# A decoder layer with a mixture of experts on one core: the residual rebuilt on VectorE in the first unit, rooms for the embedding kept a few at a time, the router's bias later

## The chip, the cores and the metric

The kernel runs on one core of a Trainium2 chip, as one program. The time is device microseconds of one execution; lower is better. Besides the timed executions one execution was run under the profiler, and every row below comes from that one.

## What is computed

One layer over 512 tokens of width 1024, all in float32. The part that matters here is the second half:

```python
x = layer_norm(alpha * x + merged @ w_o[i], ln1_g[i], ln1_b[i])
moe_out = hierarchical_moe(x, w_rg[i], b_rg[i], w_re[i], b_re[i], w_eg[i], w_eu[i], w_ed[i])
ple = jax.nn.sigmoid(x @ w_pg[i]) * (p[i] @ w_pp[i])
x = layer_norm(alpha * x + moe_out + ple, ln2_g[i], ln2_b[i])
```

Each token goes to one of 4 groups and there to 2 of 8 experts. An expert is a gated MLP, `(silu(x @ w_eg) * (x @ w_eu)) @ w_ed`, with 6 MB of weights; all 32 experts are read, about 201 MB. The term `ple` is called the embedding below: two matrix products, with w_pg (4 MB) and w_pp (1 MB), and the input p.

## The kernel before

Up to about 290 us of the profile stand the input projections, the attention and the pooling mixer; there TensorE is busy nearly all the time. Then follow three stretches.

**The output projection, the first norm and the router** (to about 380 us). The four blocks of 128 tokens are multiplied with w_o in two halves of 512 columns. The first half is scheduled by the framework, the second is in an order written by hand. The router's weights are multiplied by the norm's gain; the norm's offset becomes a bias of the router's logits, which eight narrow matmuls (`rb_ps`, L468, with the column `bcol` of the offset and the router's weights `wrr`) work out. `x1` is the normed x, kept as a high and a low half whose columns are stored in another order (`turned`); `acc` is the float32 residual to which the experts' results are added.

**The first unit** (about 377 to 417 us). A unit is a group of experts that are worked on together. KINDS = "ppppqqqpppppp": a p has 2 experts and up to 64 tokens each, a q has 4 experts and up to 32 tokens each; units are counted from 0, so units 4, 5 and 6 are the q. In a unit, `inner` multiplies the gathered tokens with w_eg (n = 0) and w_eu (n = 1), `h` is the gated product (ScalarE and VectorE, L1036 and L1037), TensorE turns it (`hT_ps`, L1050), `outer` multiplies with w_ed (L1099), `weighted` applies the gates' weights, and the scatter (L1132) adds the result to `acc`, one unit later. `gather` (L830) collects the tokens of the next two units in every second unit. In the first unit `relabel` (L731 to L741, VectorE) turns the router's tables into the experts' order; it works in the pool `lnt`, and the pool `ex`, in which `h` lives, takes the same memory, so that the first instruction on `h` waits for relabel's end. `renew` (L882) makes `acc` anew from the two halves of x1, four additions of 128x1024 on GpSimd, and ScalarE multiplies them by alpha.

**The stream of weights.** The 192 chunks of 1 MB of the experts' weights are loaded by SyncE's queue (L539), strictly in order, each into a room of 8 KB per partition; before a load is issued, the chunk that held the room must have been used by its last matmul. In the steady state there are 14 rooms: 8 of the kind s8 and 6 others. `eload_past` hands the rooms of used chunks on to the next loads.

**The embedding** borrows s8 rooms. `kept` counts those that were not handed on, up to the limit `keep`:

```python
            if tag == "s8" and kept[0] < keep[0]:
                kept[0] += 1
            elif tag != "acc":
                free.append(tag)
```

The limit is set to 8 at the start of unit 3. The generator `embedding` is advanced by `embed(i)` at six places of a unit, 0 to 5: after the first halves of the two `inner` (0 and 2), after the first product on h (1), ahead of `outer` (3), in its middle (4) and at the end (5). The table EMB gives how many steps each place takes. Steps 1 to 6 load p, add x1's halves into float32 rows (`xf`, GpSimd) and turn both; then come four quarters, each a split of the weights (`pgh` on ScalarE, `pgl` on GpSimd, L1179 and L1180; the next quarter's load is issued behind it) and four matrix steps of 30 matmuls (`pg_ps`). After unit 6 all rooms are handed back.

Of the kernel before, what the change touches and what calls it, by code (L numbers as in the profile page):

```python
# [31 lines left out]
ALPHA = 2.0 ** 0.25  # L32
# [4 lines left out]
def layer_kernel(ctx: ExitStack, tc: tile.TileContext, x, p, w_in, w_pool, pool_scale, w_pu, w_au,  # L37
                 w_o, ln1_g, ln1_b, w_rg, b_rg, w_re, b_re, w_eg, w_eu, w_ed, w_pg, w_pp,
                 ln2_g, ln2_b, out):
    nc = tc.nc  # L40
# [314 lines left out]
    with tc.manual_schedule():  # L355
# [12 lines left out]
        for k, eng in zip(range(4), (nc.vector, nc.gpsimd, nc.vector, nc.gpsimd)):  # L368
            hi, lo = (t[:, k] for t in first)
# [36 lines left out]
    for half in range(2):  # L406
        for br, (w, ah, al) in enumerate(((wpu, poh, pol), (wau, aoh, aol))):
            hi, lo = wnext()
            for c in range(4):
# [4 lines left out]
                o = mm()  # L414
# [17 lines left out]
    x1, acc = {}, {}  # L432
# [10 lines left out]
    lnt = lnt_cm.__enter__()  # L443
# [19 lines left out]
    nc.sync.dma_start(gcol, ln1_g[0].rearrange("(k p) -> p k", p=128))  # L463
    nc.sync.dma_start(bcol, ln1_b[0].rearrange("(k p) -> p k", p=128))

    o = tt("rb_ps")
    for k in range(KD):
        nc.tensor.matmul(o[:, :36], bcol[:, k:k + 1].to_broadcast([128, 128]), wrr[:, k], start=k == 0,  # L468
                         stop=k == KD - 1)

    lbias = lnt.tile([128, 40], F32, name="lbias")
    nc.vector.memset(lbias, -3.0e38)
    nc.vector.tensor_add(lbias[:, :4], rbias[:, :4], o[:, :4])
    nc.vector.tensor_add(lbias[:, 8:], rbias[:, 4:], o[:, 4:36])
    nc.vector.tensor_mul(wrr, wrr, gcol[:, :, None].to_broadcast([128, KD, 36]))
    wr2 = lnt.tile([128, KD, 72], F32R, name="wr2")
    nc.scalar.activation(wr2[:, :, :36], wrr, AF.Copy)
    nc.vector.tensor_sub(wr2[:, :, 36:], wrr, wr2[:, :, :36].bitcast(F32))
    fold = lnt.tile([128, 40], F32, name="fold")
    nc.vector.memset(fold, 0.0)  # L480
    nc.vector.tensor_add(fold[:, :4], ident[:, :4], ident[:, 36:40])
    nc.vector.tensor_add(fold[:, 8:], ident[:, 4:36], ident[:, 40:72])
# [269 lines left out]
    def residual(tb, half, o):  # L752
        cs = slice(half * 512, (half + 1) * 512)
        nc.vector.scalar_tensor_tensor(acc[tb][:, cs], acc[tb][:, cs], ALPHA, o[tb], op0=OP.mult, op1=OP.add)
        nc.vector.bn_stats(stats[:, tb, half], acc[tb][:, cs])
# [44 lines left out]
            out_proj(tb, 0, o, parts, range(4 * kk, 4 * kk + 4))  # L800
    for tb in range(NT):
        residual(tb, 0, o)
    o = [mm() for _ in range(NT)]
    parts = [wnext() for _ in range(2)]
    eload_first(8)
# [71 lines left out]
    def renew(b):  # L877

        new_acc(b)
        for tb in (b, b + 1):  # L880
            hi, lo = (x1[tb][:, i].rearrange("p (k m) -> p m k", k=KD).bitcast(F32) for i in range(2))
            nc.gpsimd.tensor_add(acc[tb].rearrange("p (m k) -> p m k", k=KD), hi, lo)  # L882

    def inner(j, n, o, ks):

# [10 lines left out]
    with tc.manual_schedule():  # L896
# [107 lines left out]
    def pair(j, other, extra):  # L1004
# [5 lines left out]
        def embed(i):  # L1010
            for _ in range(extra[i]):
                next(emb)

        h = ex.tile([128, FE], F32, name="h", bufs=1)

# [34 lines left out]
            nc.tensor.transpose(hp[:, f * 128:(f + 1) * 128], h[:, f * 128:(f + 1) * 128], ident)  # L1050
        hT = ex.tile([128, 4, 128], F32, name="hT", tag="h", bufs=1)
        nc.scalar.activation(hT, hp.rearrange("p (f s) -> p f s", f=4), AF.Copy)
        if j == 0:
            renew(2)
            for tb in range(NT):
                nc.scalar.activation(acc[tb], acc[tb], AF.Copy, scale=ALPHA)
        if last:
            split_acc(1)
        elif not four:
# [76 lines left out]
    def embedding():  # L1136
# [5 lines left out]
                nc.sync.dma_start(r, w[:, :, cs])  # L1142
            return raw

        def rows(tb):
            xf = s8([128, D], F32, "xf")
            nc.gpsimd.tensor_add(xf, x1[tb][:, 0].bitcast(F32), x1[tb][:, 1].bitcast(F32))
            return xf

        assert kept[0] >= 3  # L1150
        pr = s8([128, NT, 256], F32, "pr")
        nc.sync.dma_start(pr, p[0, 0].rearrange("(b t) c -> t b c", t=128))
        xf = [rows(tb) for tb in range(2)]
# [82 lines left out]

    EMB = {3: (0, 0, 0, 0, 0, 1), 4: (1, 1, 1, 1, 1, 2), 5: (1, 2, 1, 2, 1, 2), 6: (1, 2, 1, 2, 1, 2)}
    with tc.manual_schedule():  # L1240
# [123 lines left out]
```

## Time and profile before

| what | value |
|---|---|
| median of 3 runs (lowest, highest) | 905.2 us (904.72, 906.07) |
| the profiled execution, and its span | 910.67 us, 908.9 us |
| TensorE busy | 834.2 us (92%) |
| VectorE, ScalarE, GpSimd busy | 424.9, 216.0, 206.5 us |
| read from HBM | 239 MB, 265 GB/s over the span |
| granted TensorE clock, mean | 0.957 of full |

The profiled execution took 5.5 us longer than the median of the runs; the span is what the rows cover. TensorE is busy by far the longest, but busy says little where it runs at the lower clock (1.0 in the rows is 2.4 GHz, 0.5 is 1.2 GHz) or waits in short pieces between the chunks of the weights.

### The profile page before, as it was taken

Reading aid. Unit: us, or ns where it says so; the run is one execution under the profiler, and the core shown is the slowest. Engines: PE = TensorE matmul, PEld = TensorE weight load, DVE = VectorE, ACT = ScalarE, POOL = GpSimd, SP = SyncE. Lnnn points to the kernel's source line nnn. Section 1 sums busy time; section 2 is a strip of 40 time slices with the busy share of each in tenths; the row PEclk is TensorE's granted clock in tenths of the full one; section 3 lists DMA queues with packets and bytes.
Section 4 is the critical chain, followed back from the end, with each engine's and each line's share of the span. In section 5 each row is a group of like instructions: output and inputs, shape, how many; then the busy total and the mean of one; then the engine's idle time right before and its main releaser. Section 6 shows DMA issues by size and latency. Waiting matters only on the chain.

```text
span 908.9 us, 11416 instructions
## 1 busy us (share of the span) xinstructions
PE 834.2 (92%) x4382; PEld 528.0 (58%) x4382; DVE 424.9 (47%) x701; ACT 216.0 (24%) x447; POOL 206.5 (23%) x180
## 2 busy tenths in 40 slices
PE   8999898999999997849999988989879999999993
PEld 6886676677778786613644523657547454553642
DVE  4278557454468559581544332121121334423447
ACT  3124345444451125111110212101210110010124
POOL 3333233232312327260002202120321000000045
PEclk9999999999999898779999989999998999999997
DMA  7431312122215876457998699999997999999962
GB/s 243 138 93 48 88 52 82 58 60 80 90 50 197 263 288 241 173 234 304 420 410 346 235 414 416 408 408 419 377 420 313 419 419 419 418 420 420 420 245 95
DMA packets 65786, 241.87 MB, mean 266 GB/s; under 512 B 12096, under 2 KB 32576, under 8 KB 41408
## 3 DMA queue, kind: packets, MB, share of 16 engines
q1 hardware_dynamic: 65728, 241.10, 68.4%
q8 instruction: 36, 0.59, 0.3%
q14 instruction: 22, 0.18, 0.1%
HBM read 238.99 MB, written 2.10 MB: 265 GB/s over the span
## 4 chain that ended last, share of the span: by engine, by line
PE 44%; DMA 7%; issue 3%; POOL 1%; DVE 1%; ACT 1%; SPq 0%; POOLq 0%; ACTq 0%; DVEq 0%
PE mm L891 17%; PE mm L1099 10%; PE sc_ps L1132 5%; PE xg_ps L830 5%; DMA ew<-in_w_eu_dram 2%; DMA ew<-in_w_ed_dram 2%; PE pg_ps L142 2%; PE pg_ps L143 2%; PE pg_ps L144 2%; DMA ew<-in_w_eg_dram 2%; POOL pgl L1180 1%; DMA pr<-in_p_dram 1%; PE hT_ps L1050 1%; PE gt_ps L870 1%; ACT pgh L1179 0%
## 5 line engine op out<-in xcount | busy, mean ns | idle before, releaser
L891 PE MATMUL mm<-ew,xg 128*64 128x512 f32 (+1 forms) x1024 | 195.4, 604 | 9.1 <-DMA ew<-in_w_eu_dram 7.7
L891 PEld LDWEIGHTS mm<-ew,xg 128*64 128x64 f32 (+1 forms) x1024 | 58.0, 128 | 132.0 <-issue 112.3
L1099 PE MATMUL mm<-ew,hT 128*64 128x512 f32 (+1 forms) x512 | 100.0, 605 | 2.9 <-DMA ew<-in_w_ed_dram 2.0
L131 POOL TENSOR_TENSOR wlo<-wraw,whi 128x1024 fp32r<-128x1024 f32 x23 | 68.5, 2978 | 108.7 <-DVE whi L126 52.1
L142 PE MATMUL mm<-xth,whi 128*128 128x512 f32 x224 | 91.6, 409 | 0.0
L144 PE MATMUL mm<-xth,wlo 128*128 128x512 f32 x224 | 88.6, 396 | 0.0
L143 PE MATMUL mm<-xtl,whi 128*128 128x512 f32 x224 | 88.3, 394 | 0.0
L1037 DVE TENSOR_TENSOR h<-mm,h 128x512 f32<-128x512 f32 x26 | 18.0, 692 | 132.4 <-PE mm L891 69.4
L830 PEld LDWEIGHTS xg_ps<-G,x 128*128 128x128 f32 x448 | 57.6, 202 | 11.4 <-issue 7.4
L1133 DVE TENSOR_TENSOR acc<-acc,sc_ps 128x512 f32<-128x512 f32 x96 | 59.6, 681 | 5.6 <-PE sc_ps L1132 5.0
L1099 PEld LDWEIGHTS mm<-ew,hT 128*64 128x64 f32 (+1 forms) x512 | 27.8, 128 | 59.0 <-issue 52.1
L830 PE MATMUL xg_ps<-G,x 128*128 128x256 f32 (+1 forms) x448 | 60.9, 296 | 0.0
L1121 POOL TENSOR_TENSOR accl<-acc,acch 128x512 fp32r<-128x512 f32 x8 | 10.9, 1384 | 164.8 <-ACT acch L1120 164.8
L142 PEld LDWEIGHTS mm<-xth,whi 128*128 128x128 f32 x224 | 42.7, 191 | 9.5 <-issue 0.9
L144 PEld LDWEIGHTS mm<-xth,wlo 128*128 128x128 f32 x224 | 42.7, 190 | 9.4
L143 PEld LDWEIGHTS mm<-xtl,whi 128*128 128x128 f32 x224 | 43.0, 192 | 8.8 <-issue 0.5
L1200 DVE TENSOR_TENSOR sg<-pg_ps,sg 128x256 f32<-128x256 f32 x16 | 6.8, 425 | 83.3 <-ACT sg L1199 83.3
L143 PE MATMUL pg_ps<-pgl,xT 128*128 128x256 f32 x128 | 38.1, 298 | 7.3 <-POOL pgl L1180 7.3
L126 DVE CAST whi<-wraw 128x2048 fp32r<-128x2048 f32 x22 | 26.9, 1225 | 34.1 <-PE mm L143 16.6
L1132 PE MATMUL sc_ps<-yh,Gt 128*128 128x512 f32 x96 | 40.6, 423 | 1.6 <-DVE sg L1200 1.6
L142 PE MATMUL pg_ps<-pgh,xT 128*128 128x256 f32 x128 | 38.8, 303 | 2.5 <-ACT pgh L1179 2.5
L131 DVE TENSOR_TENSOR wlo<-wraw,whi 128x1024 fp32r<-128x1024 f32 x23 | 38.8, 1686 | 1.0
(270 smaller groups left out, 1372.3 us busy)
## 6 DMA issues: line engine op xcount, KB each, us to landing
ew<-in_w_eg_dram SPq DMA_DIRECT2D x64, 1024.0 KB, 11.6
ew<-in_w_eu_dram SPq DMA_DIRECT2D x64, 1024.0 KB, 12.3
ew<-in_w_ed_dram SPq DMA_DIRECT2D x62, 1024.0 KB, 13.5
wraw<-in_w_in_dram SPq DMA_DIRECT2D x15, 1024.0 KB, 5.5
wraw<-in_w_o_dram SPq DMA_DIRECT2D x4, 1024.0 KB, 5.1
pgr<-in_w_pg_dram SPq DMA_DIRECT2D x4, 1024.0 KB, 14.5
wraw<-in_w_pu_dram SPq DMA_DIRECT2D x2, 1024.0 KB, 5.1
wraw<-in_w_au_dram SPq DMA_DIRECT2D x2, 1024.0 KB, 5.0
```

Source lines behind the costliest of these rows:

```text
L126: nc.vector.tensor_copy(hi, wraw[i])
L131: eng.tensor_sub(lo[:, j], wraw[i][:, j], hi[:, j].bitcast(F32))
L142: nc.tensor.matmul(o, lh, rh, start=start, stop=False)
L143: nc.tensor.matmul(o, lh, rl, start=False, stop=False)
L144: nc.tensor.matmul(o, ll, rh, start=False, stop=stop)
L830: nc.tensor.matmul(o[:, kx * 256:kx * 256 + n], x1[tb][:, i, cs], G[tb // 2][:, tb % 2].rearrange("p u s -> p (u s)"), start=whole and tb ...
L891: nc.tensor.matmul(o[i * c:(i + 1) * c], xgs[j][:, k, i * c:(i + 1) * c], ew[chunk0[j] + ne * (2 * n + k // 4) + i][:, k % 4], start=k == ...
L1037: nc.vector.tensor_mul(ht, o, ht)
L1099: nc.tensor.matmul(o[i * n:(i + 1) * n], hT[:, f, i * n:(i + 1) * n], ew[chunk0[j] + ne * (4 + f // 2) + i][:, f % 2, halves[c]], start=f ...
L1121: nc.gpsimd.tensor_sub(l, acc[tb][:, halves[c]], h.bitcast(F32))
L1132: nc.tensor.matmul(o, Gt[:, tb * 128:(tb + 1) * 128], y[c][i], start=i == 0, stop=i == 1)
L1133: nc.vector.tensor_add(acc[tb][:, cs], acc[tb][:, cs], o)
```

## The change

Three things. The router's bias and folded weights are written behind the first half of the output projection instead of ahead of it. `renew` adds on VectorE, and both its calls and the multiplication by alpha stand together in unit 0, behind the tables `Gw` and ahead of `outer`. The embedding keeps its rooms by a table KEEP, in steps from the end of unit 2 on; `xf` takes one room for two blocks; the table EMB deals the 26 steps out in another way.

```diff
-    o = tt("rb_ps")
-    for k in range(KD):
-        nc.tensor.matmul(o[:, :36], bcol[:, k:k + 1].to_broadcast([128, 128]), wrr[:, k], start=k == 0,
-                         stop=k == KD - 1)
...
     for tb in range(NT):
         residual(tb, 0, o)
+
+    ob = tt("rb_ps")
+    for k in range(KD):
+        nc.tensor.matmul(ob[:, :36], bcol[:, k:k + 1].to_broadcast([128, 128]), wrr[:, k], start=k == 0,
+                         stop=k == KD - 1)
...
-            nc.gpsimd.tensor_add(acc[tb].rearrange("p (m k) -> p m k", k=KD), hi, lo)
+            nc.vector.tensor_add(acc[tb].rearrange("p (m k) -> p m k", k=KD), hi, lo)
...
         relabel(rk, weigh())
-        renew(0)
...
             for _ in range(extra[i]):
                 next(emb)
+            keep[0] = KEEP.get((j, i), keep[0])
...
-        if j == 0:
-            renew(2)
-            for tb in range(NT):
-                nc.scalar.activation(acc[tb], acc[tb], AF.Copy, scale=ALPHA)
...
         if not last:
             Gw = weights_of(j)
+        if j == 0:
+            for b in (0, 2):
+                renew(b)
+                for tb in (b, b + 1):
+                    nc.scalar.activation(acc[tb], acc[tb], AF.Copy, scale=ALPHA)
...
-        def rows(tb):
-            xf = s8([128, D], F32, "xf")
-            nc.gpsimd.tensor_add(xf, x1[tb][:, 0].bitcast(F32), x1[tb][:, 1].bitcast(F32))
-            return xf
+        def rows(b):
+            xf = s8([128, 2, D], F32, "xf")
+            for i in range(2):
+                nc.gpsimd.tensor_add(xf[:, i], x1[b + i][:, 0].bitcast(F32), x1[b + i][:, 1].bitcast(F32))
+            return [xf[:, i] for i in range(2)]
...
-    EMB = {3: (0, 0, 0, 0, 0, 1), 4: (1, 1, 1, 1, 1, 2), 5: (1, 2, 1, 2, 1, 2), 6: (1, 2, 1, 2, 1, 2)}
+    EMB = {3: (0, 0, 0, 1, 0, 0), 4: (1, 1, 1, 1, 1, 1), 5: (2, 2, 1, 2, 2, 1), 6: (2, 2, 1, 2, 1, 1)}
+
+    KEEP = {(2, 5): 2, (3, 3): 4, (3, 5): 5, (4, 0): 6, (4, 1): 7, (4, 2): 8}
...
-            if j in (min(EMB), NU - 2):
+            if j == NU - 2:
                 keep[0] = 8
```

What this does to the order is shown at three places. The first is VectorE in unit 0, behind the products on `h`; `Gt` is the turned table of the gates, which the scatter needs. Before:

```order
L741 TENSOR_TENSOR ranked<-by_slot 128x128
L1037 TENSOR_TENSOR h<-mm,h 128x512 x2
L862 TENSOR_TENSOR Gw<-iota_c,posm 128x512
L864 TENSOR_TENSOR Gw<-Gw,comb 128x512
L873 TENSOR_SCALAR Gt<-gt_ps 128x512
```

And now:

```order
L1037 TENSOR_TENSOR h<-mm,h 128x512 x2
L862 TENSOR_TENSOR Gw<-iota_c,posm 128x512
L864 TENSOR_TENSOR Gw<-Gw,comb 128x512
L882 TENSOR_TENSOR acc<-x_2688 128x1024
L882 TENSOR_TENSOR acc<-x_2742 128x1024
L882 TENSOR_TENSOR acc<-x_2925 128x1024
L882 TENSOR_TENSOR acc<-x_2928 128x1024
L873 TENSOR_SCALAR Gt<-gt_ps 128x512
```

The four additions left GpSimd, where they stood directly ahead of the first `xf`, and stand on VectorE ahead of `Gt`.

The second is SyncE's queue at the turn from unit 3 to unit 4. ew_3618 is chunk 55, the next two are chunks 56 and 57, the first of unit 4's w_eu; in brackets is whose counters a row waits for (DMAHW are earlier DMAs). Before:

```order
L539 DMA ew_3618<-in_w_eg_dram 128x2048 [waits DMAHW6_49,PE_49]
L539 ISA
L539 DMA ew_3744<-in_w_eu_dram 128x2048 [waits DMAHW7_49,PE_49]
L539 ISA
L539 DMA ew_3746<-in_w_eu_dram 128x2048 [waits DMAHW0_49,PE_49]
L1152 DMA pr_3786<-in_p_dram 128x4x256 [waits DMAHW1_49]
L539 ISA
L539 DMA ew_3818<-in_w_eu_dram 128x2048 [waits DMAHW2_49,PE_49]
```

And now:

```order
L521 DMA ew_3618<-in_w_eg_dram 128x2048 [waits DMAHW6_49,PE_49]
L521 ISA
L521 DMA ew_3628<-in_w_eu_dram 128x2048 [waits DMAHW7_49]
L521 ISA
L521 DMA ew_3630<-in_w_eu_dram 128x2048 [waits DMAHW0_49]
L1154 DMA pr_3683<-in_p_dram 128x4x256 [waits DMAHW1_49,PE_49]
L521 ISA
L521 DMA ew_3753<-in_w_eu_dram 128x2048 [waits DMAHW2_49,PE_49]
```

The order is the same, but chunks 56 and 57 no longer wait for TensorE; chunks 58 and 59 now wait for what 56 and 57 waited for (the last `outer` of unit 3).

The third is ScalarE in unit 6, where the last quarter of the embedding's weights is split. Before:

```order
L1036 ACTIVATE h<-mm 128x512
L1199 ACTIVATE sg<-pg_ps 128x256 x3
L1052 ACTIVATE hT<-hT_ps 128x512
L1179 ACTIVATE pgh<-pgr 128x2048
L1179 ACTIVATE pph<-ppr 128x512
L1199 ACTIVATE sg<-pg_ps 128x256 x4
```

And now:

```order
L1036 ACTIVATE h<-mm 128x512
L1204 ACTIVATE sg<-pg_ps 128x256 x2
L1184 ACTIVATE pgh<-pgr 128x2048
L1184 ACTIVATE pph<-ppr 128x512
L1052 ACTIVATE hT<-hT_ps 128x512
L1204 ACTIVATE sg<-pg_ps 128x256 x4
```

The split moved from behind `hT` to ahead of it, into the middle of the second `inner`. On TensorE the eight narrow matmuls `rb_ps` moved behind 25 more matmuls of the output projection.

## Rows read from the trace of the kernel before

**Rows 1.** The page, the span in 40 equal slices of 22.7 us: GB/s that the DMA engines moved.

```profile
GB/s 243 138 93 48 88 52 82 58 60 80 90 50 197 263 288 241 173 234 304 420 410 346 235 414 416 408 408 419 377 420 313 419 419 419 418 420 420 420 245 95
```

**Rows 2.** Windows: length, busy us (count) of PE, PEld, DVE, ACT, POOL; clock; DMA; GB/s.

```profile
300.00:309.60 9.60, 9.57 (x43) 7.59 (x41) 4.93 (x11) 0.00 (x0) 3.44 (x1) 1.00 0.65 135
...
312.00:319.00 7.00, 7.00 (x23) 5.94 (x23) 2.97 (x7) 1.39 (x2) 2.45 (x1) 0.51 1.03 423
...
394.00:405.60 11.60, 0.00 (x0) 0.02 (x1) 10.57 (x8) 0.60 (x1) 8.29 (x3) 0.65 0.49 206
...
495.00:510.00 15.00, 15.00 (x100) 9.95 (x96) 6.00 (x13) 1.15 (x3) 0.00 (x0) 1.00 0.25 81
...
528.00:541.00 13.00, 9.03 (x32) 1.59 (x32) 2.23 (x4) 0.20 (x1) 0.00 (x0) 0.74 1.01 422
...
685.00:695.00 10.00, 10.00 (x77) 7.23 (x77) 0.42 (x1) 0.38 (x1) 0.73 (x1) 0.88 0.51 178
700.00:860.00 160.00, 160.00 (x854) 81.63 (x855) 58.52 (x100) 17.42 (x34) 1.47 (x2) 1.00 1.01 419
```

**Rows 3.** The chain that ended last, in order of time: start us, us, what.

```profile
407.38 5.44 PE mm L1099 x16
...
413.40 3.58 PE mm L1099 x16
...
670.36 3.57 PE mm L891 x32
```

**Rows 4.** Timeline of TensorE at the router's bias, with the idle time before it.

```profile
311.26 2.89 PE L468 MATMUL rb_ps<-wrr,bcol 128*128 128x36 f32 x16 [1.68 <-DMA bcol<-in_ln_b_dram]
```

**Rows 5.** Timeline of the first unit, 383 to 406 us, all engines.

```profile
383.33 10.52 PE L891 MATMUL mm<-ew,xg 128*64 128x512 f32 x48
...
386.69 0.42 DVE L731 TENSOR_TENSOR by_rank<-oh,rk 128x256 f32<-128x256 f32 x1
...
387.11 15.19 POOL L882 TENSOR_TENSOR acc<-x 128x1024 f32<-128x1024 f32 x4 [18.11 <-DVE by_rank L731]
...
387.48 3.69 DVE L734 TENSOR_TENSOR by_slot<-oh,posm 128x256 f32<-128x256 f32 x1
...
391.54 3.50 DVE L737 TENSOR_TENSOR by_rank<-iota_e,r 128x256 f32<-128x256 f32 x1
...
395.08 3.73 DVE L740 TENSOR_TENSOR by_slot<-by_rank,s 128x256 f32<-128x256 f32 x1
398.84 3.60 DVE L741 TENSOR_TENSOR ranked<-by_slot 128x128 f32<-128x128 f32 x1
...
402.94 0.29 DVE L741 TENSOR_TENSOR ranked<-by_slot 128x128 f32<-128x128 f32 x1
403.39 0.60 ACT L1036 ACTIVATE h<-mm 128x512 f32<-128x512 f32 x1 [18.59 <-issue]
404.02 1.49 DVE L1037 TENSOR_TENSOR h<-mm,h 128x512 f32<-128x512 f32 x2 [0.79 <-ACT h L1036]
...
405.61 1.08 PE L1050 MATMUL hT_ps<-ident,h 128*128 128x128 f32 x4 [11.75 <-issue]
```

**Rows 6.** SyncE's queue at the turn to unit 4: start, us of issuing, loads.

```profile
472.46 15.38 SPq L539 DMA_DIRECT2D ew<-in_w_eg_dram  x8
506.24 0.90 SPq L539 DMA_DIRECT2D ew<-in_w_eu_dram  x2
```

**Rows 7.** Timelines of TensorE and GpSimd at the last split, 672 to 690 us.

```profile
677.98 0.38 PE L142 MATMUL pg_ps<-pgh,xT 128*128 128x256 f32 x1 [2.48 <-ACT pgh L1179]
682.61 0.58 PE L143 MATMUL pg_ps<-pgl,xT 128*128 128x256 f32 x1 [4.25 <-POOL pgl L1180]
688.42 1.92 PE L1099 MATMUL mm<-ew,hT 128*32 128x512 f32 x16
...
678.06 4.50 POOL L1180 TENSOR_TENSOR pgl<-pgr,pgh 128x2048 fp32r<-128x2048 f32 x1 [7.68 <-ACT pgh L1179]
```

**Rows 8.** VectorE's additions: groups with the mean, or min/median/max, ns of one.

```profile
L792 DVE TENSOR_TENSOR x<-acc,x 128x512 fp32r<-128x512 f32 x1 | 1.0, 1044 | 0.0
...
L131 DVE TENSOR_TENSOR wlo<-wraw,whi x23: 1173/1226/3424, 18.6 to 320.1; 128x1024 fp32r<-128x1024 f32 x23
```

More of the change, by code (lines that the diff above doesn't have):

```diff
@@ L464, in layer_kernel @@
     nc.sync.dma_start(bcol, ln1_b[0].rearrange("(k p) -> p k", p=128))
-    o = tt("rb_ps")
-    for k in range(KD):
-        nc.tensor.matmul(o[:, :36], bcol[:, k:k + 1].to_broadcast([128, 128]), wrr[:, k], start=k == 0,
-                         stop=k == KD - 1)
[L471 to L482, printed above, removed]
     weg = w_eg[0].rearrange("g e (p k) f -> (g e) p k f", p=128)
@@ L802, in layer_kernel @@
         residual(tb, 0, o)
+    ob = tt("rb_ps")
+    for k in range(KD):
+        nc.tensor.matmul(ob[:, :36], bcol[:, k:k + 1].to_broadcast([128, 128]), wrr[:, k], start=k == 0,
+                         stop=k == KD - 1)
+    lbias = lnt.tile([128, 40], F32, name="lbias")
+    nc.vector.memset(lbias, -3.0e38)
+    nc.vector.tensor_add(lbias[:, :4], rbias[:, :4], ob[:, :4])
+    nc.vector.tensor_add(lbias[:, 8:], rbias[:, 4:], ob[:, 4:36])
+    nc.vector.tensor_mul(wrr, wrr, gcol[:, :, None].to_broadcast([128, KD, 36]))
+    wr2 = lnt.tile([128, KD, 72], F32R, name="wr2")
+    nc.scalar.activation(wr2[:, :, :36], wrr, AF.Copy)
+    nc.vector.tensor_sub(wr2[:, :, 36:], wrr, wr2[:, :, :36].bitcast(F32))
+    fold = lnt.tile([128, 40], F32, name="fold")
+    nc.vector.memset(fold, 0.0)
+    nc.vector.tensor_add(fold[:, :4], ident[:, :4], ident[:, 36:40])
+    nc.vector.tensor_add(fold[:, 8:], ident[:, 4:36], ident[:, 40:72])
     o = [mm() for _ in range(NT)]
@@ L1143, in load @@
             return raw
-        def rows(tb):
-            xf = s8([128, D], F32, "xf")
-            nc.gpsimd.tensor_add(xf, x1[tb][:, 0].bitcast(F32), x1[tb][:, 1].bitcast(F32))
-            return xf
-        assert kept[0] >= 3
+        def rows(b):
[3 more added lines that the diff above has]
+            return [xf[:, i] for i in range(2)]
+        assert kept[0] >= 2
         pr = s8([128, NT, 256], F32, "pr")
         nc.sync.dma_start(pr, p[0, 0].rearrange("(b t) c -> t b c", t=128))
-        xf = [rows(tb) for tb in range(2)]
+        xf = rows(0)
         yield
-        assert kept[0] >= 6
+        assert kept[0] >= 4
         pT = s8([128, 2, 2, S], F32R, "pT")
@@ L1166, in embedding @@
         for tb in range(NT):
+            assert kept[0] >= (5, 6, 6, 7)[tb]
+            if tb == 0:
+                xf += rows(2)
             xt = s8([128, 2, KD, 128], F32R, "xT")
             xT.append(xt)
-            split_transpose(xt, xf.pop(0))
-            if tb + 2 < NT:
-                xf.append(rows(tb + 2))
+            split_transpose(xt, xf[tb])
+            if tb % 2:
+                xf[tb - 1] = xf[tb] = None
             if tb < NT - 1:
```

## The prediction

> **What bounds the kernel now.** I read the slices of the page first, for the stream of weights. From slice 17 on (386 us) the DMA engines move some 419 GB/s, and slices 21, 22, 27 and 30 show holes in that [rows 1]. Then the windows, for what TensorE does meanwhile. From 700 to 860 us both are full: 160.00 of 160 us busy at clock 1.00, and 419 GB/s [rows 2]. A chunk of 1 MB (1.049 million bytes) takes 1.049/0.419 = 2.50 us, so the 12 chunks of a unit of two experts take 30 us, and TensorE, which keeps pace without idle time, needs about the same. In that stretch nothing in the change can win or lose. It ends sooner only if it begins sooner for both, TensorE and the stream. Between 309 and 700 us I looked for places where one of them stood still, and found four that the change touches:
>
> - The wait for the router's bias: TensorE idle for 1.68 us [rows 4], then the clock at 0.51 from 312 to 319 us [rows 2].
> - The end of the first unit: TensorE idle from 394 to 405.6 us, 0.00 of 11.6 us [rows 2], and the first half of `outer` behind it slow, 5.44 us where the second half takes 3.58 [rows 3].
> - A hole in the stream from 495 to 510 us, 81 GB/s [rows 2]. TensorE is busy there; it pays later, when the chunks are late: 9.03 of 13 us busy and clock 0.74 from 528 to 541 us, the stream full at 422 GB/s [rows 2].
> - The last split of the embedding's weights: TensorE idle for 2.48 and 4.25 us [rows 7], and behind it a second hole in the stream, 178 GB/s from 685 to 695 us [rows 2].
>
> **The change part by part.**
>
> *Router's bias.* The eight matmuls do the same work 25 matmuls later. The column they wait for had landed at 311.26 us [rows 4]; the matmuls of that kind ahead of it take 9.57/43 = 0.22 us each [rows 2], so they now come up 25 x 0.22 = 5.5 us after 309.6, at about 315 us, and wait for nothing. That takes away 1.68 us, and if the clock then stays up, 7.00 x (1 - 0.51) = 3.4 us: 5.1 us together. The lower bound is 1.7 us, if the narrow matmuls themselves bring the clock down. I take 5, because the low stretch begins just behind the idle time. The Trainium skill, "TensorE: Matmul & The Clock Gate" (Part 1, What's actually happening), says that the granted clock follows how busy the engine has lately been, which speaks for 5.1 and against 1.7; that the fall follows the wait in this trace agrees. Queued behind the eight on TensorE is only the output projection; the weights made from them are next needed by the router some 15 us later, and VectorE has the room for them.
>
> *The rebuild off GpSimd.* In rows 5 relabel on VectorE goes slow when GpSimd begins the four additions (387.11 us, 15.19 us in all): the additions and products of it take 3.69, 3.50, 3.73 and 3.60 us, each about as long as one addition on GpSimd (15.19/4 = 3.8), where the same forms take 0.42 (three) and 0.29 us (the last) when undisturbed. The excess is 14.52 - 3 x 0.42 - 0.29 = 13.0 us. The first instruction on `h` starts at 403.39, 0.16 us behind relabel's end. Without the excess that is 390.4 us; `h` is done on ScalarE at 391.0 and its first product at 391.7. The second product now waits for TensorE, whose `inner` ends at 383.33 + 10.52 = 393.85 [rows 5]: done at about 394.7, and TensorE turns `h` at 394.8 instead of 405.61. That is 10.8 us. If the clock no longer falls, the first half of `outer` wins another 5.44 - 3.58 = 1.9 us: 12.7 at most. TensorE still idles some 2.7 us here, more than the 1.68 us that brought the clock down above, so I take 11.5, with 10.8 as the lower bound. The first load behind this point waits for that `outer`, so the stream begins again as much sooner.
>
> *The rebuild on VectorE.* No row shows it there. From below, one is 1.2 us (median of 128x1024, contiguous); from above 2.1, twice the 1.04 us of the half-width addition that writes with the same stride [rows 8]; if the stride cost VectorE what it costs GpSimd, 3.8. Four are 4.9 to 8.4, at worst 15.2 us. They start at about 396.2, so `Gt` and the row sums behind them are ready by 402.5 to 406, at worst 413 us. TensorE needs them for the scatter, which stands behind the rest of `outer` (to about 404) and both `inner` of unit 1, some 13.9 us: 418 us. The cost on the path is nothing even at the worst; if that cover were gone it would be the 4.9 to 8.4 us. ScalarE's four products wait in line with the additions, and the next `h` is not due before 411.
>
> *Rooms.* SyncE issued unit 4's eight w_eg chunks by 487.8 us and then stood until 506.24 [rows 6], when the last `outer` of unit 3 freed a room, because all of unit 3's s8 rooms were kept. In the new order chunks 56 and 57 follow chunk 55 with no wait for TensorE, and 58 and 59 take over the old wait. The stream is two chunks further when the hole ends: 2 x 2.50 = 5.0 us. The hole itself is 15 x (1 - 81/419) = 12.1 us, so some 7 remain. The bounds are 2.5 (one chunk) and 5.5. The loads of the embedding's weights move behind three chunks, 7.5 us, and are not needed until the end of unit 4.
>
> *The steps dealt out anew.* The matrix steps are the same 16. The split that TensorE waited for (from its last matmul on `h` to 682.61 us; the clock is back at 687.5) now has the second half of an `inner` (3.57 us, [rows 3]), scatters and the turning of `h` between it and its first user, together about 6.5 us, against 1.9 us on ScalarE and 4.50 on GpSimd [rows 7]. The wait goes, and with it the late `outer` at 688.42 that made the hole of 10 x (1 - 178/419) = 5.8 us. Against that, one more matrix step (30 matmuls of 0.12 us, 3.6 us) now stands ahead of that `outer`. So 2.2 to 5.8 us; I take 4.5. The split at the end of unit 5 keeps its place and its wait.
>
> *Sum.* 5 + 11.5 + 5 + 4.5 = 26 us. The profiled execution would take 910.67 - 26 = 884.7 us; against the median of the runs, 5.5 us lower, 905.2 - 26 = **879 us**. All four move the stream as well as TensorE, so they add up. The bounds: 1.7 + 10.8 + 2.5 + 2.2 = 17.2 us, 888; and 5.1 + 12.7 + 5.5 + 5.8 = 29.1 us, to which up to 4 us come if TensorE, which wins the waits of the last split beyond what the stream does, comes closer to it at the end: 872.
>
> **The rivals.**
>
> *Only the early parts pay.* Then the new table frees two chunks early and pays for it in unit 5, which now has eight matrix steps. For it: the 7 us that remain of the hole, and fewer steps in unit 4, where TensorE waits for chunks anyway. Against it: the order shows the two loads without a wait. 5 + 11.5 = 16.5 us, 889 us.
>
> *The end does not move.* From 700 us on both are full, so if the stream were bound to its old times, all would be given back as waits for chunks. For it: 419 GB/s to the end. Against it: the stream starts again behind `outer` of unit 0, which moves. 905 us, no change.
>
> *Slower, by the clock.* The change puts less of the matrix steps into unit 4, where chunks come every 2.5 us and TensorE waits between them; in 528 to 541 us that had it at 0.74. If it stayed at half through units 4 to 6, which hold some 150 us of work at full clock in 195 us of stream (78 chunks at 2.50 us), they would take 300 us, 105 more: 984. It decides from the point where the half clock lasts long enough to use up the 45 us of slack and the 26 won, over 70 us of full-speed work. Against it: 700 to 860 us at 1.00, and the low stretch at 528 to 541 ended with the waits. The Trainium skill, "TensorE: Matmul & The Clock Gate" (HAM oscillation), describes a kernel whose waits for DMA keep the clock down in that way; the 0.74 agrees with it, but nothing here shows it lasting.
>
> **How the numbers follow.** The forecast has 0.72, only the early parts 0.18, no move of the end 0.06, slower 0.04. Its own range is 872 to 888; with the first rival 872 to 889, widened by 1 us below for the spread of the runs: 871 to 889. It leaves out the last two cases and the edges, 2 in 10. About 0.2% is what a measurement of this kernel can tell from no change. Faster by more than that: 0.72 + 0.18 = 0.90; the same 0.06; slower 0.04.
>
> **What would show it.** In the profile of the changed kernel: no idle time of TensorE ahead of `rb_ps`, and clock 1.00 behind it; relabel's products at 0.42 us, and `h` turned within 1.5 us of the end of `inner`; GpSimd free there, four additions on VectorE of 1.2 to 2.1 us; SyncE's issue of chunk 56 right behind chunk 55, and a hole of about 7 us split in two; GB/s at 419 from unit 4 to the last chunk, without the dip that stood at 685 us. Wrong it would be if `h` still waited for something else in the memory that it takes over, if the router's chain between 350 and 377 us ate the first 5 us, or if a kept room held up the stream elsewhere.

## The result, and the profile after

The changed kernel takes 881.34 us (median of 4 runs, 880.99 to 882.05), the kernel before 905.63 beside it: 24.3 us by the medians. The ratio of the runs is 0.9715 with a 95% interval of 0.969 to 0.9741, which is 25.8 us. In a second comparison the medians were 881.36 and 908.02, 26.7 us apart, and the ratio 0.9705 (0.9677 to 0.9734), 26.8 us. The forecast was 879 us (871 to 889). The profiled execution has 882.05 us, a span of 880.3 and a mean granted clock of 0.972.

I went through the same four places. The wait for the router's bias first; timeline of TensorE, then windows (columns as in [rows 2]):

```profile
307.86 0.39 PE L144 MATMUL mm<-whi,merged 128*128 128x512 f32 x1
...
313.53 1.87 PE L788 MATMUL rb_ps<-wrr,bcol 128*128 128x36 f32 x16
315.23 0.48 PE L142 MATMUL mm<-whi,merged 128*128 128x512 f32 x1
...
312.00:319.00 7.00, 7.00 (x40) 6.05 (x39) 5.28 (x10) 1.50 (x2) 3.51 (x1) 1.00 1.03 430
```

No idle time is noted ahead of `rb_ps`, the eight matmuls take 1.87 us in place of 2.89 [rows 4], and 312 to 319 us is at clock 1.00, where it was 0.51 [rows 2]. The old place of the eight lies 25 matmuls further up, ahead of the one that begins at 307.86 us. In the kernel before that one was due at 309.42: the wait begins at 311.26 - 1.68 = 309.58 [rows 4] with the end of a matmul of 0.39 us, and such matmuls begin 0.23 us apart. The end of `inner` of unit 0 is at 387.21 and was at 393.85 [rows 5]. So of the 6.6 us by which this end is earlier, some 1.5 lay ahead of the change and belong to the two executions, and 5.1 are the change's. The size depends on the execution: the profile of the changed kernel run again gives 6.6 us by the same sum (rb_ps at 314.21, end of `inner` at 386.35).

The end of the first unit; timelines of VectorE, TensorE and ScalarE, and the group of the four additions (min/median/max ns):

```profile
380.84 0.41 DVE L716 TENSOR_TENSOR by_slot<-oh,posm 128x256 f32<-128x256 f32 x1
...
383.31 0.29 DVE L723 TENSOR_TENSOR ranked<-by_slot 128x128 f32<-128x128 f32 x1
...
387.29 0.69 DVE L1037 TENSOR_TENSOR h<-mm,h 128x512 f32<-128x512 f32 x1 [2.20 <-PE mm L891]
...
389.22 9.21 DVE L882 TENSOR_TENSOR acc<-x 128x1024 f32<-128x1024 f32 x4
398.20 0.83 DVE L873 TENSOR_SCALAR Gt<-gt_ps 128x512 fp32r<-128x512 f32 x1
...
376.69 10.52 PE L891 MATMUL mm<-ew,xg 128*64 128x512 f32 x48
388.08 0.63 PE L1050 MATMUL hT_ps<-ident,h 128*128 128x128 f32 x4 [0.87 <-issue]
389.39 3.65 PE L1100 MATMUL mm<-ew,hT 128*64 128x512 f32 x16 [0.69 <-ACT hT L1052]
...
410.88 0.50 PE L1133 MATMUL sc_ps<-yh,Gt 128*128 128x512 f32 x1
...
383.76 0.60 ACT L1036 ACTIVATE h<-mm 128x512 f32<-128x512 f32 x1 [5.60 <-DVE ranked L723]
...
L882 DVE TENSOR_TENSOR acc<-x x4: 2304/2388/2501, 389.2 to 395.9; 128x1024 f32<-128x1024 f32 x4
```

Relabel's products are back at 0.41 and 0.29 us (3.5 to 3.7 in [rows 5]), it ends at 383.31 + 0.29 = 383.60 us, 3.6 us ahead of the end of `inner` (376.69 + 10.52 = 387.21), the second product of `h` waits for TensorE and not for memory, and TensorE stands for 0.87 us where it stood for 11.75. The first half of `outer` takes 3.65 us where it took 5.44; the second half took 3.58 [rows 3]. The rebuild costs VectorE 9.21 us, and `Gt` behind it is there at 399 us, long before its scatter at 410.88.

The stream of weights; the page's 40 slices (of 22.0 us), windows, and SyncE's queue:

```profile
GB/s 251 141 98 49 48 96 48 96 48 96 48 49 190 199 392 240 181 312 408 406 421 385 282 418 417 410 407 383 385 386 418 420 419 420 418 420 420 420 243 98
...
480.00:500.00 20.00, 20.00 (x154) 11.45 (x154) 6.79 (x12) 4.07 (x9) 4.73 (x2) 1.00 0.69 246
...
600.00:625.00 25.00, 21.95 (x173) 16.19 (x172) 4.73 (x9) 5.40 (x9) 7.58 (x5) 0.93 0.94 361
640.00:660.00 20.00, 20.00 (x156) 12.31 (x158) 6.99 (x12) 4.03 (x6) 7.75 (x5) 1.00 0.95 381
660.00:840.00 180.00, 177.73 (x948) 89.44 (x940) 62.31 (x106) 19.53 (x38) 1.74 (x3) 1.00 1.01 419
...
456.86 11.21 SPq L521 DMA_DIRECT2D ew<-in_w_eg_dram  x6
468.28 0.86 SPq L521 DMA_DIRECT2D ew<-in_w_eu_dram  x2
470.59 0.39 SPq L1154 DMA_DIRECT2D pr<-in_p_dram  x1
486.47 8.97 SPq L521 DMA_DIRECT2D ew<-in_w_eu_dram  x5
```

Chunks 56 and 57 are issued at 468.28 us, right behind chunk 55, and the next ones take the old wait, until 486.47. From 480 to 500 us the hole is 20 x (1 - 246/419) = 8.3 us, but the stream stays low for longer than that, and in the kernel before it did so beyond the 495 to 510 us of [rows 2]. The window 470 to 530 us holds the whole hole in both (the kernel before, then the changed one):

```profile
470.00:530.00 60.00, 57.88 (x350) 27.56 (x346) 25.08 (x44) 9.01 (x17) 9.50 (x4) 1.00 0.81 319
```

```profile
470.00:530.00 60.00, 54.27 (x353) 26.85 (x350) 27.49 (x47) 12.14 (x21) 10.02 (x5) 0.94 0.91 356
```

It was 60 x (1 - 319/419) = 14.3 us of the stream and is 60 x (1 - 356/419) = 9.0: 5.3 us less, some two chunks. The dip at the last split (178 GB/s, [rows 2]) is gone; two shallower ones stay, 25 x (1 - 361/419) = 3.5 us and 20 x (1 - 381/419) = 1.8. Here the split of the last quarter is hidden: GpSimd makes it from 642.28 to 646.85 us and TensorE is busy for 20.00 of 20 us from 640 to 660. The split of quarter 2 still has a wait (timelines of GpSimd and TensorE):

```profile
642.28 4.57 POOL L1185 TENSOR_TENSOR pgl<-pgr,pgh 128x2048 fp32r<-128x2048 f32 x1 [0.65 <-DMA ew<-in_w_eu_dram]
...
618.41 0.39 PE L143 MATMUL pg_ps<-pgl,xT 128*128 128x256 f32 x1 [3.05 <-POOL pgl L1185]
```

### The profile page after: what moved, and what is told of

The parts are those of the page before. It is cut to its first block, busy times and chain, and to the rows that moved or that the text cites. A ratio compares the mean times of both kernels' runs of the same rounds, so it can differ in the third digit from the quotient of the medians.

```text
span 880.3 us, 11414 instructions
## 1 busy us (share of the span) xinstructions
PE 824.1 (94%) x4382; PEld 524.5 (60%) x4382; DVE 421.6 (48%) x705; ACT 216.8 (25%) x447; POOL 192.1 (22%) x176
## 4 chain that ended last, share of the span: by engine, by line
PE 55%; DMA 9%; DVE 3%; POOL 2%; issue 1%; ACT 1%; SPq 1%; POOLq 0%; DVEq 0%; ACTq 0%
PE mm L891 18%; PE mm L1100 10%; PE xg_ps L830 6%; PE sc_ps L1133 5%; DMA ew<-in_w_ed_dram 4%; DMA ew<-in_w_eu_dram 3%; PE mm L142 3%; PE mm L144 3%; PE mm L143 3%; DMA ew<-in_w_eg_dram 2%; PE pg_ps L142 1%; PE pg_ps L143 1%; PE pg_ps L144 1%; PE hT_ps L1050 1%; PE gt_ps L870 1%
## 5 line engine op out<-in xcount | busy, mean ns | idle before, releaser
L891 PEld LDWEIGHTS mm<-ew,xg 128*64 128x64 f32 (+1 forms) x1024 | 60.5, 128 | 130.4 <-issue 109.0
L830 PEld LDWEIGHTS xg_ps<-G,x 128*128 128x128 f32 x448 | 57.6, 202 | 11.4 <-issue 7.4
L1122 POOL TENSOR_TENSOR accl<-acc,acch 128x512 fp32r<-128x512 f32 x8 | 10.8, 1390 | 167.7 <-ACT acch L1121 167.7
L131 DVE TENSOR_TENSOR wlo<-wraw,whi 128x1024 fp32r<-128x1024 f32 x23 | 40.7, 1769 | 1.0
L1133 PE MATMUL sc_ps<-yl,Gt 128*128 128x512 f32 x96 | 37.9, 395 | 0.0
## 6 DMA issues: line engine op xcount, KB each, us to landing
ew<-in_w_eg_dram SPq DMA_DIRECT2D x64, 1024.0 KB, 11.4
```

The lines of the kernel that those rows point to most:

```text
L131: eng.tensor_sub(lo[:, j], wraw[i][:, j], hi[:, j].bitcast(F32))
L830: nc.tensor.matmul(o[:, kx * 256:kx * 256 + n], x1[tb][:, i, cs], G[tb // 2][:, tb % 2].rearrange("p u s -> p (u s)"), start=whole and tb ...
L891: nc.tensor.matmul(o[i * c:(i + 1) * c], xgs[j][:, k, i * c:(i + 1) * c], ew[chunk0[j] + ne * (2 * n + k // 4) + i][:, k % 4], start=k == ...
L1122: nc.gpsimd.tensor_sub(l, acc[tb][:, halves[c]], h.bitcast(F32))
L1133: nc.tensor.matmul(o, Gt[:, tb * 128:(tb + 1) * 128], y[c][i], start=i == 0, stop=i == 1)
```

## The experiments

Eleven variants and the changed kernel itself were timed, each beside the kernel before, and one execution of each was profiled. They were timed in three groups, in which the kernel before had medians of 907.59 us (bias_early, renew_pool, emb_old, steps_old), 908.02 (changed again, renew_dve_old_place, only_renew, split_apart) and 908.06 (the others). So the last column compares medians across groups; by the ratios its entries would differ by up to 1.2 us (for steps_old 5.9). The first table has the times. The second has, from the profiled executions of the kernels that the text follows through the units, the start of the first turning of `h` (`hT_ps`) in a unit and of the final sums (`sum_ps`), in us. Executions of one kernel differ in it by 1 to 2 us from the first unit on, as the two lines of the changed kernel show.

| kernel | median us | ratio to before (95%) | against 881.36 |
|---|---|---|---|
| changed, again | 881.36 | 0.9705 (0.9677 to 0.9734) | |
| bias_early | 886.32 | 0.9765 (0.9739 to 0.9791) | +5.0 |
| renew_pool | 894.47 | 0.9860 (0.9837 to 0.9883) | +13.1 |
| renew_pool_new_place | 894.21 | 0.9848 (0.9823 to 0.9872) | +12.9 |
| renew_dve_old_place | 884.41 | 0.9731 (0.9703 to 0.9758) | +3.1 |
| emb_old | 890.80 | 0.9815 (0.9789 to 0.9841) | +9.4 |
| steps_old | 886.09 | 0.9770 (0.9748 to 0.9793) | +4.7 |
| only_bias | 905.28 | 0.9971 (0.9952 to 0.9989) | |
| only_renew | 896.58 | 0.9862 (0.9835 to 0.9889) | |
| split_apart | 881.68 | 0.9703 (0.9678 to 0.9729) | +0.3 |
| load_late | 880.85 | 0.9699 (0.9675 to 0.9724) | -0.5 |
| load_late_apart | 879.78 | 0.9692 (0.9667 to 0.9718) | -1.6 |

| kernel | unit 0 | unit 1 | unit 4 | unit 6 | unit 7 | sums |
|---|---|---|---|---|---|---|
| before | 405.61 | 432.62 | 543.14 | 674.90 | 722.99 | 886.0 |
| changed | 388.08 | 412.85 | 519.17 | 650.77 | 693.82 | 857.4 |
| changed, again | 387.21 | 411.99 | 517.40 | 649.47 | 692.17 | 855.7 |
| bias_early | 394.56 | 419.32 | 525.19 | 657.25 | 699.94 | 863.5 |
| renew_pool | 399.17 | 425.90 | 532.06 | 663.28 | 706.70 | 870.2 |
| emb_old | 388.45 | 413.23 | 523.51 | 655.38 | 703.17 | 866.2 |
| steps_old | 387.93 | 412.69 | 519.00 | 650.88 | 698.63 | 861.6 |
| only_bias | 398.43 | 426.52 | 535.92 | 670.03 | 718.04 | 881.1 |
| only_renew | 391.60 | 416.37 | 526.71 | 660.60 | 709.02 | 872.0 |
| load_late | 387.79 | 412.57 | 517.29 | 648.62 | 692.03 | 855.6 |
| load_late_apart | 385.88 | 410.65 | 515.09 | 647.15 | 688.05 | 852.3 |

**The changed kernel with one part taken back.** The theory is the forecast's: four parts at four places which add up. The rival says that only the early parts pay, or that early gains are given back.

*bias_early.* The eight matmuls and what follows from them stand in their old place:

```diff
+    ob = tt("rb_ps")
...
     weg = w_eg[0].rearrange("g e (p k) f -> (g e) p k f", p=128)
...
     for tb in range(NT):
         residual(tb, 0, o)
-    ob = tt("rb_ps")
...
```

> The changed kernel with only the router's bias put back ahead of the output projection; all else as changed. Four independent parts (the forecast): the wait of 1.7 us for the column and the half clock behind it come back, everything from the end of the first unit on starts about 5 us later (at most 6.6, which is what the two traces show up to the end of inner of unit 0), and so does the end: 886 to 888 us where the changed kernel has 881.3. Early gains are given back later (rival): the first unit starts 5 to 6.6 us later, but the difference shrinks at the holes of the stream further on, and the end is within 2 us of the changed kernel: 881 to 883 us. Only the idle time counts and not the clock (lower bound of the forecast): 883 us.

+5.0 us by the median, but no run lies near it: three of the six take 883.7 to 884.6 us (+2.3 to +3.2) and three 888.1 to 888.7 (+6.7 to +7.4). The profiled execution, 888.09 us, is one of the slower three. In it the wait and the half clock are back, and every unit is 6 to 6.5 us later than in the first line of the changed kernel, the sums 6.1: nothing is given back on the way. What the faster three lose less is not known, since none of them was profiled. Timeline and window:

```profile
311.12 2.97 PE L468 MATMUL rb_ps<-wrr,bcol 128*128 128x36 f32 x16 [1.66 <-DMA bcol<-in_ln_b_dram]
...
312.00:319.00 7.00, 7.00 (x23) 5.93 (x24) 2.97 (x7) 1.39 (x2) 2.51 (x1) 0.53 1.03 416
```

*renew_pool.* The additions on GpSimd, at their old places (the four products of ScalarE with them):

```diff
-            nc.vector.tensor_add(acc[tb].rearrange("p (m k) -> p m k", k=KD), hi, lo)
+            nc.gpsimd.tensor_add(acc[tb].rearrange("p (m k) -> p m k", k=KD), hi, lo)
...
         relabel(rk, weigh())
+        renew(0)
...
         nc.scalar.activation(hT, hp.rearrange("p (f s) -> p f s", f=4), AF.Copy)
+        if j == 0:
+            renew(2)
+            for tb in range(NT):
+                nc.scalar.activation(acc[tb], acc[tb], AF.Copy, scale=ALPHA)
...
-        if j == 0:
-            for b in (0, 2):
-                renew(b)
-                for tb in (b, b + 1):
-                    nc.scalar.activation(acc[tb], acc[tb], AF.Copy, scale=ALPHA)
```

> The changed kernel with the rebuild of x1 back on GpSimd and at its old two places. Four independent parts: relabel's products on VectorE take about 3.6 us each again, h is ready 11 us behind inner instead of 1, outer of unit 0 begins 10.8 to 12.8 us later, and so does the end: 892 to 894 us. Early gains are given back later: the same late unit 0, but an end of 881 to 885 us. If the four additions and products of relabel were slow for another reason than GpSimd's additions beside them, relabel would stay at 0.42 us and the end at 881 us.

+13.1 us: unit 0 is 11.1 us later, unit 1 13.05, the sums 12.8.

*emb_old* takes back the table, the limits of kept rooms and the rows made in pairs; *steps_old* the table alone:

```diff
-    EMB = {3: (0, 0, 0, 1, 0, 0), 4: (1, 1, 1, 1, 1, 1), 5: (2, 2, 1, 2, 2, 1), 6: (2, 2, 1, 2, 1, 1)}
+    EMB = {3: (0, 0, 0, 0, 0, 1), 4: (1, 1, 1, 1, 1, 2), 5: (1, 2, 1, 2, 1, 2), 6: (1, 2, 1, 2, 1, 2)}
```

> The changed kernel with the embedding's steps, rows and kept rooms as before (one set of eight rooms from unit 3 on, the old table). The forecast: 5 us for the rooms and 4.5 us for the steps are lost: 890 to 891 us, with SyncE standing before chunk 56 until outer of unit 3 and a dip of the stream at the last split. Rival 'only the early parts pay': the two are worth nothing in the end, 881 to 883 us. By the differences between the two traces at the units' starts (4.1 us at unit 4, 5.1 us from unit 6 to 7): 890.5 us.

> The changed kernel with the old table of steps alone; rooms are still kept a few at a time, and the rows of the embedding are made as changed. The forecast: the rooms' part stays (chunks 56 and 57 without a wait for TensorE, unit 4 as early as in the changed kernel), the steps' part is lost: 884 to 887 us, with the wait for the split in unit 6 and the dip of the stream behind it back. If the split in unit 6 is hidden by the new order of rooms and not by the table: 881 to 882 us. If the rooms pay only together with the table: 890 us, as with both undone.

+9.4 and +4.7 us, so 4.7 for the rooms (with the rows made in pairs) and 4.7 for the steps. SyncE's queue of emb_old, and behind it that of steps_old with TensorE's waits at the last split:

```profile
457.23 11.21 SPq L521 DMA_DIRECT2D ew<-in_w_eg_dram  x6
486.85 0.90 SPq L521 DMA_DIRECT2D ew<-in_w_eu_dram  x2
```

```profile
468.10 19.10 SPq L521 DMA_DIRECT2D ew<-in_w_eu_dram  x4
...
653.97 0.38 PE L142 MATMUL pg_ps<-pgh,xT 128*128 128x256 f32 x1 [2.48 <-ACT pgh L1184]
658.60 0.58 PE L143 MATMUL pg_ps<-pgl,xT 128*128 128x256 f32 x1 [4.25 <-POOL pgl L1185]
```

emb_old stands between the last w_eg and the first w_eu chunk of unit 4 as in [rows 6], and is 4.3 us late from unit 4 on. steps_old issues its first w_eu chunk at 468.10, is as early as the changed kernel up to unit 6, waits there the very 2.48 and 4.25 us of [rows 7], and is 4.8 us late at unit 7. Each part is lost at its place and stays lost: 'only the early parts pay' is out.

**Engine or place of the rebuild.** *renew_pool_new_place* has the additions on GpSimd at the new place in the order (the first two lines of the diff of renew_pool alone), *renew_dve_old_place* on VectorE at the old places (the rest of it).

> The changed kernel with the rebuild at its new place in the order but on GpSimd. GpSimd has nothing ahead of the additions, so they begin as soon as the rooms of acc are free, whatever their place in the program. If the engine is what counts: relabel's products go slow beside them as at the old place, 892 to 894 us. If the new place in the order is enough (GpSimd starts behind relabel): 881 to 884 us.

> The changed kernel with the rebuild on VectorE as changed, but at the two places in the order of before (two additions behind relabel, two behind the turning of h). It tells the engine from the place. If the engine is what counts: relabel stays at 0.42 us, the two additions of 2.3 us stand ahead of the second product of h and end at about 388.5, so h is turned some 1 to 2 us later than in the changed kernel: 882 to 884 us. If the place counts as much as the engine: 4.6 us or more later, 886 us or more.

The first is as slow as renew_pool, +12.9 us. Timelines of VectorE, GpSimd and TensorE:

```profile
380.73 3.69 DVE L716 TENSOR_TENSOR by_slot<-oh,posm 128x256 f32<-128x256 f32 x1
384.45 0.42 DVE L717 TENSOR_REDUCE s<-by_slot 128x8 f32<-128x256 f32 x1
384.79 3.51 DVE L719 TENSOR_TENSOR by_rank<-iota_e,r 128x256 f32<-128x256 f32 x1
...
380.36 15.18 POOL L882 TENSOR_TENSOR acc<-x 128x1024 f32<-128x1024 f32 x4 [16.66 <-DVE by_rank L713]
...
398.85 1.09 PE L1050 MATMUL hT_ps<-ident,h 128*128 128x128 f32 x4 [11.75 <-issue]
```

GpSimd has nothing ahead of the additions in its queue, so they begin behind `by_rank` whatever their place in the program. The second costs 3.1 us, a little more than the 1 to 2 expected; timelines of TensorE and VectorE:

```profile
388.50 1.09 PE L1051 MATMUL hT_ps<-ident,h 128*128 128x128 f32 x4 [2.39 <-issue]
390.27 5.97 PE L1100 MATMUL mm<-ew,hT 128*64 128x512 f32 x16 [0.69 <-ACT hT L1053]
...
382.41 4.59 DVE L882 TENSOR_TENSOR acc<-x 128x1024 f32<-128x1024 f32 x2
```

Two additions now end at 387.0, 0.9 us behind `inner`; TensorE stands for 2.39 us instead of 0.87, and the half of `outer` behind that takes 5.97 us instead of 3.65. By the medians the engine is worth 10.1 us at the old places (894.47 against 884.41) and 12.9 at the new one; the place is worth 3.1 us on VectorE and nothing on GpSimd. In the traces the place costs more at first: 1.5 us of wait, 2.3 of slower `outer` and 0.5 of slower turning.

**One part alone.** *only_bias* and *only_renew* are the kernel before with that part.

> The kernel before with only the router's bias behind the output projection. Independent parts: 5 us faster (up to 6.6), 901.5 to 903 us. If the first 5 us are given back at the holes of the stream or at the end of the first unit, which are as before: 906 to 908 us.

> The kernel before with only the rebuild moved to VectorE and behind outer's first part. The parts are independent: 11.5 us (10.8 to 12.8) faster, 892.5 to 895 us. If TensorE or the stream gave part of it back at the holes that stay (495 to 510 us and at the last split): 896 to 902 us. If the half clock behind the wait for h stays because bias and steps are as before: 10.8 us, 894.5 us.

only_renew is 11.4 us faster by the medians (12.5 by the ratio, 10.1 to 15.0), the difference that was expected; its time of 896.58 us lies above the expected 892.5 to 895, because the kernel before had 908.02 beside it and not 905. only_bias is faster by 2.8 us by the medians (2.6 by the ratio, 1.0 to 4.4): less than 5, and its 905.28 us lie between the two ranges expected. Its profiled execution ends 4.9 us ahead of that of before, but the latter (910.67 us) lies 2.6 us above the median of before in that comparison. Part of it is the size of the loss in the kernel before, which is not the same each time: the profile of only_renew, in which the early place stays, has the wait with less behind it (timeline and window).

```profile
309.72 1.95 PE L468 MATMUL rb_ps<-wrr,bcol 128*128 128x36 f32 x16 [1.81 <-DMA bcol<-in_ln_b_dram]
...
312.00:319.00 7.00, 7.00 (x25) 5.58 (x25) 5.12 (x8) 1.50 (x2) 2.42 (x1) 0.76 1.03 429
```

That is 1.81 + 7 x (1 - 0.76) = 3.5 us instead of 5.1. Whether something is also given back when one part stands alone stays open. The unit starts of only_bias are 7.2 us ahead of before at unit 4 and 4.9 at unit 6, and those of only_renew 16.4 and 14.3; in emb_old, which has both parts, they are 19.6 and 19.5. But two executions of the changed kernel differ by 1.8 and 1.3 us there.

**The dip that stayed at 600 to 625 us.** The wait of 3.05 us for the split of quarter 2 looked like its cause. *split_apart* puts an `inner` between that split and its user:

```diff
-    EMB = {..., 6: (2, 2, 1, 2, 1, 1)}
+    EMB = {..., 6: (0, 2, 3, 2, 1, 1)}
```

> The changed kernel with one row of the table altered: in unit 6 the matrix steps stand two places later (0, 2, 3, 2, 1, 1 in place of 2, 2, 1, 2, 1, 1), so that a whole inner lies between the split at the end of unit 5 and its first user. The changed kernel has TensorE idle there for 3.05 us and the clock at half behind it until 622.8 us, with the stream at 361 GB/s from 600 to 625 us. If that wait delays the stream and the end as the one of unit 6 did in the kernel before: 2 to 4 us faster, 877 to 879 us. If the stream makes up for it, or the steps crowd later in unit 6: 881 to 882 us, no change.

No change in time. The wait for the split is gone from the trace, but TensorE waits for chunks at the same place instead (1.44 and 1.50 us ahead of `inner` at 618 and 621 us), and the stream is as low (388 GB/s, where the changed kernel run again had 389). SyncE's queue in the changed kernel shows the cause:

```profile
592.43 17.66 SPq L521 DMA_DIRECT2D ew<-in_w_eg_dram  x8
618.39 0.57 SPq L1143 DMA_DIRECT2D pgr<-in_w_pg_dram  x1
619.63 0.40 SPq L1143 DMA_DIRECT2D ppr<-in_w_pp_dram  x1
620.28 15.24 SPq L521 DMA_DIRECT2D ew<-in_w_eu_dram  x8
```

From 610.1 to 618.4 us the load of the last quarter stands at the head, until GpSimd has split quarter 2 out of the room it needs, and the w_eu chunks stand behind it. *load_late* moves that load one step back; *load_late_apart* has this and the row of split_apart.

```diff
-            if q < 3:
+            if q < 2:
                 raw = load(q + 1)
             yield
+            if q == 2:
+                raw = load(q + 1)
```

> The changed kernel with the load of the last quarter of the embedding's weights moved one step back, behind four w_eu chunks on SyncE. In the changed kernel SyncE stands from 610 to 618 us with that load at its head, until GpSimd has split quarter 2 and so freed its room, and the w_eu chunks queued behind it land late: 320 to 361 GB/s around 615 to 625 us. Theory (the dip comes from SyncE's queue): the four w_eu chunks are issued right behind the w_eg chunks, the dip is gone or at 410 GB/s and more from 600 to 625 us, and the end is 1.5 to 3.5 us earlier, 878 to 880 us. Rival (the dip comes from TensorE, which stands 3 us for the split and frees rooms late): dip and time stay, 881 to 882 us. A third way: the load of the last quarter now lands too late for its split, and unit 6 pays: 882 to 885 us.

> Both together: the load of the last quarter behind the w_eu chunks (here behind all eight, since its step comes later), and the matrix steps of unit 6 two places later, so that TensorE doesn't wait for the split of quarter 2. If SyncE's queue and TensorE's wait each hold back the stream: 2 to 5 us faster than the changed kernel, 876 to 879 us. If only the queue counts: like the kernel with the late load alone. If neither does: 881 to 882 us.

SyncE's queue and two windows of load_late, and behind them a window of the changed kernel and one of load_late_apart:

```profile
613.30 2.95 SPq L521 DMA_DIRECT2D ew<-in_w_eu_dram  x4
616.63 0.57 SPq L1143 DMA_DIRECT2D pgr<-in_w_pg_dram  x1
617.87 7.74 SPq L1143 DMA_DIRECT2D ppr<-in_w_pp_dram  x1
630.78 3.18 SPq L521 DMA_DIRECT2D ew<-in_w_eu_dram  x4
...
600.00:625.00 25.00, 21.95 (x173) 16.19 (x173) 4.30 (x8) 5.01 (x8) 7.24 (x4) 0.93 1.00 411
625.00:640.00 15.00, 14.47 (x116) 9.98 (x119) 4.18 (x8) 3.15 (x5) 2.22 (x3) 1.00 0.99 371
```

```profile
625.00:640.00 15.00, 14.47 (x117) 11.00 (x116) 2.82 (x5) 1.41 (x4) 1.86 (x3) 1.00 1.01 413
```

```profile
600.00:625.00 25.00, 21.98 (x165) 11.22 (x164) 5.79 (x10) 5.23 (x8) 6.53 (x3) 1.00 1.00 410
```

The cause is shown: with the load moved, four chunks go out at 613.30 and the dip at 600 to 625 us is gone, 411 GB/s, with TensorE's wait still there. But it comes back behind the moved load: the other four chunks are issued only at 630.78, and 625 to 640 us has 371 GB/s where the changed kernel has 413. So it buys almost nothing: from unit 0 to the sums load_late takes 467.8 us, the changed kernel 469.3 and 468.5. Both edits together take 466.4, with the gain between unit 6 and unit 7 (40.9 us, against 43.1, 42.7 and, with the load alone, 43.4). The row of split_apart alone has 40.8 us there too, but it pays for that with 72.7 us from unit 5 to unit 6, where both edits together have 69.5 and the changed kernel 69.7. The times agree in direction, but their intervals overlap: load_late_apart, the fastest of all kernels here by its median, is not shown to beat the changed kernel.

## Why the prediction was right, by its own steps

**Router's bias: 5 forecast.** 5.1 and 6.6 in the traces; when taken back +5.0 by the median, of runs that lose 2.3 to 3.2 or 6.7 to 7.4; 2.6 (1.0 to 4.4) alone. The bounds of 1.7 and 5.1 were set by whether the clock falls with the narrow matmuls or with the wait. At the new place the same matmuls leave it at 1.00, so they alone do not bring it down; at the old place, behind the wait, it fell in all three profiles. What wait and fall cost differs by execution, 3.5 us in only_renew and 5.1 in the kernel before. The 5 was read from an execution 5.5 us above the median, and one part alone shows about half of it: as the price of a usual execution the term was too high.

**The rebuild off GpSimd: 11.5 forecast, 10.8 to 12.7.** Between the end of `inner` and unit 1's `hT_ps` the changed kernel is quicker by (432.62 - 393.85) - (412.85 - 387.21) = 13.1 us, and taking it back costs 13.1. Of the former, 10.9 are idle time (11.75 to 0.87), 1.8 the first half of `outer` and 0.45 the turning (1.08 to 0.63). This term was mis-sized by 1.6 us: I expected the idle time that stays to bring the clock down. The 2.7 us that the forecast called idle counted the 1.08 us of the turning itself, which is work. The idle time was 0.87 and 0.69 us with the turning of `h` between, and the half of `outer` behind it ran at 3.65 us; behind 2.39 us, in renew_dve_old_place, it took 5.97. The cause, VectorE's products held up by GpSimd's additions, is shown by renew_pool_new_place. The Trainium skill, "SBUF — State Buffer" (Who interferes with whom), says that a VectorE instruction with two inputs in that memory contends with a GpSimd instruction that reads it, and that a reduction doesn't. The trace agrees: 3.69 and 3.51 us for products, 0.42 for the reduction between them.

**The rebuild on VectorE: 1.2 to 2.1 us each forecast, 3.8 at worst.** 2.39 us (median), outside the range that I took but inside the worst case. It cost the path nothing, as said: `Gt` stood ready 12 us before its use.

**Rooms: 5.0 forecast, 2.5 to 5.5.** 4.2 us between units 3 and 4 in the traces (23.97 ahead at unit 4, 19.77 at unit 1 and unchanged at unit 3), 4.7 by emb_old and steps_old. In the ten profiles with the new rooms the stretch from unit 3 to unit 4 is 44.6 to 46.7 us, in the four with the old ones 49.8 to 50.9. The hole shrank by 5.3 us, some two chunks as forecast; the forecast had measured it too short, 12.1 us where the window that holds all of it gives 14.3, so 9.0 remain and not 7.

**The steps: 4.5 forecast.** 5.0 us between units 6 and 7 in the traces, 4.7 by steps_old.

**The sum.** Taking parts back one by one gives 5.0 + 13.1 + 9.4 = 27.5 us; the whole change is 24.3 and 26.7 by the medians of the two comparisons (25.8 and 26.8 by the ratios), the forecast was 26. So the parts add up within the measurement. That the total fits better than its terms is in part luck: the forecast subtracted from the median terms that it had read in an execution 5.5 us slower, and the rebuild, put too low, made up for some of the bias, put too high. From profiled execution to profiled execution the gain is 910.67 - 882.05 = 28.6 us. Of the rivals, 'only the early parts pay' fell with emb_old; the end moved by as much as unit 7 did (28.6 and 29.2 us in the profiled executions), so the stream was not bound to its old times; and 600 to 625, 640 to 660 and 660 to 840 us are at clock 0.93, 1.00 and 1.00, so the half clock did not last. One step was wrong: no dip was to be left from unit 4 on. I had credited the dips to TensorE's waits alone and not looked at what stands in SyncE's queue behind the embedding's loads. Two readings of [rows 1] in the forecast are off as well, though no term uses them: counted from 0, the slices are at some 419 GB/s from 19 on (about 432 us) and not from 17, and the hole called 27 is slice 28.

## What to carry to other kernels

Find the stretches in which both the bounding engine and the stream of weights are full; time can be won only ahead of them, and gains won there add up as long as both begin earlier. When a short instruction on one engine takes many times its usual duration, look for what another engine does in just that span: the remedy here was the engine, and the place in the program made no difference to an engine with an empty queue. A load that waits for its room at the head of an in-order queue delays every load behind it; but removing a dip is worth nothing where the next dip takes it up.

## What the runs showed of the hardware

- The addition of two 128x1024 halves that are read 512 bytes apart costs VectorE 2.39 us, where 128x1024 contiguous is 1.23 [rows 8]; GpSimd takes 3.80 for it (15.19/4, [rows 5]), with relabel's products on VectorE beside it. The Trainium skill, "SBUF — State Buffer" (Door 1: The DMA port swizzle), says that accesses which each fall in a new short line of that memory pay a penalty; the factor of 1.9 agrees in direction.
- A wait of TensorE of the same length need not cost the same: behind 1.66 us 312 to 319 us had clock 0.53, behind 1.81 us, in another execution, 0.76.
